# Feed-forward stages of a hybrid decoder step: from a scheduled order to a chain of slots in source order

## The chip, the cores and the metric

One core of a Trainium2 chip. The metric is the device time of one execution in microseconds (us), the median of the runs shown; lower is better.

## What is computed

One decoder layer for 1024 prompt tokens and 8 sampled tokens (1032 columns, D_MODEL = 1024, D_FF = 2816), in float32. The layer is a pair of half-step feed-forward stages around a mixer (attention and a state-space scan) and a cross attention:

```python
def swiglu(x, w_gate, w_up, w_down):
    return (jax.nn.silu(x @ w_gate) * (x @ w_up)) @ w_down

x = x + 0.5 * swiglu(rms_norm(x, g_ffn1), w1_gate, w1_up, w1_down)
...
x = x + 0.5 * swiglu(rms_norm(x, g_ffn2), w2_gate, w2_up, w2_down)
```

The change touches the two feed-forward stages alone.

## The kernel before

Everything lies transposed: features on the partitions, tokens on the free axis. The 1032 tokens are cut into P0 and P1 of 388 and a rest R of 256. `ffn` (both stages call it) walks through the 22 hidden blocks of 128 in pairs: a **gate-up unit** for an even block m, one for the odd block m + 1, then a **down unit** that adds both blocks into the residual x. The last pair has no down unit of this kind: `down_last` does it.

Each matrix product is made in Strassen's (Winograd's) form over P0 and P1: seven products of 388 columns instead of eight, on the weight matrices A11, A12 (gate weights), A21, A22 (up weights) and the sums S1 to S4 of them, with the factors B11 to B22 and T1 to T4 of the activations. The rest R is multiplied plainly by the four A matrices. Each product is made of three float32r matmuls (`three`): high half times high half, high times low, low times high. So a product of a gate-up unit is 12 matmuls of 388 columns, the rest of one matrix 12 matmuls of 256; a pair of blocks with its down unit has 396 matmuls: 252 of 388 columns and 144 of 256.

A weight matrix goes this way: `raw_` loads 512 KB by a DMA on SP's queue into a ring of two tiles (`fraw`); `add_up` makes the sums on DVE (VectorE); `split` copies the high half on ACT (ScalarE) and takes the low half by a subtraction, in turn on DVE and POOL (GpSimd), into a ring of four tiles (`fw`). Results lie in two sets of four PSUM banks (`fb`), which units take in turn: three banks of P0 and P1 products (b1, b2, b3) and one of the rest. `evac` says what becomes of a bank. The **seed** is one of these: ACT copies b1 to b2 after A11's product, so that b2 goes on from it, while b1 goes on with A12's product; both must wait for the copy. The hidden activations are made by SiLU on ACT and a product on DVE, put into halves by `put` (ACT copy, then a subtraction on DVE or POOL), and read by the down unit as its factors.

The order on each engine is the work of a scheduler, which goes by its own timing; the order in the source is a preference. The order of products is the table ORDER: A11, S2, A12, S3, S1, S4, A22, A21; a down unit takes the table's rows in the order 0, 7, 4, 1, 2, 3, 5, 6 for two halves c of the columns, each with two bank sets in step.

Of the kernel before, what the change touches and what calls it, by code (L numbers as in the profile page):

```python
# [10 lines left out]
F32 = mybir.dt.float32  # L11
# [65 lines left out]
def tile_step(ctx, tc, a, o):  # L77
# [237 lines left out]
    def split(hl, src, like=lambda t: t):  # L315

        hi, lo = like(hl[0]), like(hl[1])
        st["turn"] = not st.get("turn")
        nc.scalar.copy(hi, src)  # L319
        (nc.vector if st["turn"] else nc.gpsimd).tensor_sub(lo, src, hi.bitcast(F32))  # L320
        return hl
# [19 lines left out]
    def ffn(x, F, wg, wu, wd, fin, turn, mid=None):  # L341
# [27 lines left out]
        def gate_up(m):  # L369
            q = m % 2  # L370
            g_, u_ = raw_(cols_of(wg, m * 128)), raw_(cols_of(wu, m * 128))
            t = {"A11": g_[:, :512], "A12": g_[:, 512:], "A21": u_[:, :512], "A22": u_[:, 512:]}
            bk, rb = bank_set()
            b1, b2, b3 = bk
            sums = sums_of(m)
            e = {}

            def mat(name):
                if name == "S2":
                    add_up("S1", t, sums[:, :512])  # L380
                if name in SUMS and name not in t:
                    add_up(name, t, sums[:, :512] if name == "S3" else sums[:, 512:1024])
                return split(two(512), t[name])

            def rest(name, w):
                i = name in ("A21", "A22")
                first, last = name in ("A11", "A22"), name in ("A12", "A21")
                for j in range(4):
                    three(rb[:, int(i)], w, j, F["R"][j + (4 if name in ("A12", "A22") else 0)], first and j == 0, last and j == 3)

            def rest_end():
                gr, hr = u1_(NR), u1_(NR)
                nc.scalar.activation(gr, rb[:, 0], AF.Silu)
                nc.vector.scalar_tensor_tensor(hr, rb[:, 1], 0.5, gr, op0=OP.mult, op1=OP.mult)
                put(Hd["R"][q], hr, nc.vector)

            def evac(name):
                if name == "A11":
                    nc.scalar.copy(b2, b1)
                elif name == "S2":  # L400
                    e["U2"] = acc_(PA)
                    nc.scalar.copy(e["U2"], b2)
                elif name == "A12":
                    e["g0"] = g1_(PA)
                    nc.scalar.activation(e["g0"], b1, AF.Silu)
                elif name == "S3":
                    e["U3"] = acc_(PA)
                    nc.scalar.copy(e["U3"], b2)  # L408
                elif name == "S1":
                    e["u1"] = sq_(PA)  # L410
                    nc.vector.tensor_add(e["u1"], b3, e["U3"])  # L411
                elif name == "S4":
                    g1, u1 = g1_(PA), e["u1"]
                    nc.vector.tensor_add(g1, b3, e["U2"])
                    nc.scalar.activation(g1, g1, AF.Silu)
                    nc.vector.scalar_tensor_tensor(u1, u1, 0.5, g1, op0=OP.mult, op1=OP.mult)
                    if Hd["plain"]:
                        put(Hd["B22" if q else "B12"], u1, nc.vector)
                    elif q:
                        b12, t1 = Hd["b"]  # L420
                        nc.vector.tensor_sub(t1, u1, t1)
                        put(Hd["T2"], t1, nc.vector)
                        put(Hd["B22"], u1, nc.gpsimd)
                        nc.vector.tensor_sub(b12, u1, b12)
                        put(Hd["T3"], b12, nc.gpsimd)
                elif name == "A22":
                    u0, u1 = sq_(PA), e["u1"]
                    nc.vector.scalar_tensor_tensor(u0, b2, 0.5, e["g0"], op0=OP.mult, op1=OP.mult)
                    put(Hd["B21" if q else "B11"], u0, nc.vector)
                    if Hd["plain"]:  # L430
                        pass
                    elif q:
                        t2 = Hd["b"][1]
                        nc.vector.tensor_sub(u0, u0, t2)
                        put(Hd["T4"], u0, nc.gpsimd)
                    else:
                        nc.vector.tensor_sub(u0, u1, u0)
                        put(Hd["T1"], u0, nc.gpsimd)
                        Hd["b"] = (u1, u0)

            late = m == 0
            early = {}
            for name, b, f, first in ORDER:
                if late and name == "A21":
                    continue
                if name == "S3":
                    early["S1"] = mat("S1")
                w = early.pop(name, None) or mat(name)
                if f:
                    for j in range(4):  # L450
                        three(bk[b], w, j, F[f][j], first and j == 0, j == 3)
                if f:
                    evac(name)
                if name[0] == "A" and not late:
                    rest(name, w)
            if late:
                for name in ("A11", "A12", "A22", "A21"):
                    rest(name, mat(name))
            rest_end()

        def down(m0):
            ra, rb_ = (raw_(wd[m * 128:(m + 1) * 128]) for m in (m0, m0 + 1))
            sums = sums_of(1)
            twice = lambda t: t.rearrange("p (i c) -> p i c", i=2)
            for c in range(2):
                cs = slice(c * 256, (c + 1) * 256)
                wa, wb = twice(ra)[:, :, cs], twice(rb_)[:, :, cs]
                t = {"A11": wa[:, 0], "A21": wa[:, 1], "A12": wb[:, 0], "A22": wb[:, 1]}
                W = {}

                def pair(names, src):
                    hi, lo = split(two(512), src, twice if len(src.shape) == 3 else (lambda x: x))
                    for i, name in enumerate(names):
                        W[name] = hi[:, i * 256:(i + 1) * 256], lo[:, i * 256:(i + 1) * 256]

                def need(name):
                    if name in W:
                        return
                    if name in ("A11", "A21"):
                        pair(("A11", "A21"), wa)  # L480
                    elif name in ("A12", "A22"):
                        pair(("A12", "A22"), wb)
# [11 lines left out]
                def evac(name, e):  # L494
# [15 lines left out]
                    elif name == "A22":  # L510
                        add(xb[:, P0], xb[:, P0], b2)
# [1283 lines left out]
```

## Time and profile before

| | us |
|---|---|
| median of 3 runs (2667.94 to 2682.07) | 2678.17 |
| the profiled execution | 2680.7 |
| its span, first to last instruction | 2678.6 |
| PE busy in the span | 2508.9 (94%) |
| PE weight loads busy | 2384.3 (89%) |
| DVE, ACT, POOL busy | 1806.0, 1172.3, 906.3 |

The first feed-forward stage takes about 104 to 800 us of the span, the second about 1945 to 2640 us; between them lie the mixer and the cross attention. Times are microseconds from the start of the span. Matmuls overlap in the records: one of 388 columns is shown with 0.34 us, but the next starts sooner, so the pitch from start to start counts. Line numbers L... are those of the kernel before.

### The profile page before, as it was taken

The page shows a single profiled execution, that of the slowest core. Times are in us where ns is not written, and L with a number is a line of the kernel's source. Part 1 is how long each engine was busy: PE and PEld are TensorE (multiplying, and loading weights), DVE is VectorE, ACT ScalarE, POOL GpSimd, SP SyncE. Part 2 cuts the span into 40 slices and gives each one's busy share as a digit, 9 for nine tenths or more (in the row PEclk, how much of TensorE's full clock was granted, in tenths as well). Part 3 has the DMA queues.
Part 4 walks back from the last instruction along what each step waited for, and adds up shares of the span by engine and source line. Part 5 has one row for each costly group of instructions (what it writes and reads, how often), then busy time and mean ns, then how long its engine had stood idle before and what let it go on. Part 6 is the DMA issues. An engine that isn't in the chain of part 4 may idle for free.

```text
span 2678.6 us, 42139 instructions
## 1 busy us (share of the span) xinstructions
PE 2508.9 (94%) x15999; PEld 2384.3 (89%) x15999; DVE 1806.0 (67%) x3660; ACT 1172.3 (44%) x2415; POOL 906.3 (34%) x675
## 2 busy tenths in 40 slices
PE   6899999999999999999797899989699999999998
PEld 5899999999998899999576899978689999999997
DVE  8566666666656777778568877564876666666665
ACT  5443333333334455554467623333343333333345
POOL 5433333333334111115156564102443333333333
PEclk9999999999999999999898999999899999999999
DMA  5411111111113222327657634573011111111112
GB/s 172 135 50 64 57 57 58 61 59 57 57 48 112 81 70 65 92 75 239 201 167 221 221 108 132 169 236 104 23 48 48 48 48 49 55 48 52 51 48 80
DMA packets 273747, 252.12 MB, mean 94 GB/s; under 512 B 17392, under 2 KB 243880, under 8 KB 273536
## 3 DMA queue, kind: packets, MB, share of 16 engines
q1 hardware_dynamic: 271872, 249.34, 30.2%
q8 instruction: 126, 2.06, 0.3%
q14 instruction: 77, 0.63, 0.1%
q10 hardware_dynamic: 1672, 0.09, 0.0%
HBM read 204.25 MB, written 49.98 MB: 95 GB/s over the span
## 4 chain that ended last, share of the span: by engine, by line
PE 70%; DVE 15%; DMA 7%; issue 3%; ACT 3%; POOL 1%; SPq 0%; DVEq 0%; ACTq 0%; POOLq 0%
PE fb L332 44%; PE pqkv L245 5%; PE pxbc L245 4%; PE pcq L245 3%; DMA fraw<-in_w_up_dram 2%; PE pco L245 2%; PE pwa L245 1%; DVE fs L366 1%; PE pwo L245 1%; PE po L1071 1%; PE ps L1045 1%; PE ptr L1065 1%; PE pd L245 1%; PE pzz L245 1%; PE cps L1604 1%
## 5 line engine op out<-in xcount | busy, mean ns | idle before, releaser
L235 POOL TENSOR_TENSOR wl<-wr,wh 128x1024 fp32r<-128x1024 f32 (+4 forms) x79 | 166.1, 2103 | 562.1 <-ACT wh L231 537.2
L320 POOL TENSOR_TENSOR fw<-fraw,fw 128x512 fp32r<-128x512 f32 x131 | 174.2, 1330 | 465.8 <-ACT fw L319 392.4
L320 POOL TENSOR_TENSOR fw<-fs,fw 128x512 fp32r<-128x512 f32 x128 | 172.3, 1346 | 400.4 <-ACT fw L319 347.2
L319 ACT CAST fw<-fs 128x512 fp32r<-128x512 f32 x256 | 158.2, 618 | 268.5 <-PE fb L332 152.5
L319 ACT CAST fw<-fraw 128x512 fp32r<-128x512 f32 x262 | 162.2, 619 | 189.6 <-PE fb L332 185.9
L366 DVE TENSOR_TENSOR fs<-fraw 128x512 f32<-128x512 f32 (+1 forms) x168 | 101.0, 601 | 141.7 <-DMA fraw<-in_w_up_dram 67.0
L320 DVE TENSOR_TENSOR fw<-fraw,fw 128x512 fp32r<-128x512 f32 x131 | 102.5, 782 | 110.9 <-ACT fw L319 110.6
L320 DVE TENSOR_TENSOR fw<-fs,fw 128x512 fp32r<-128x512 f32 x128 | 95.5, 746 | 99.1 <-ACT fw L319 99.1
L332 PE MATMUL fb<-hRh,fw 128*128 128x256 f32 x640 | 137.3, 280 | 0.5
L231 ACT CAST wh<-wr 128x1024 fp32r<-128x1024 f32 (+1 forms) x80 | 76.8, 960 | 99.4 <-PE pqkv L245 23.4
L332 PEld LDWEIGHTS fb<-hRh,fw 128*128 128x128 f32 x640 | 109.2, 188 | 3.7 <-DVE x L516 3.7
L245 PE MATMUL pxbc<-xh,wh 128*128 128x344 f32 x288 | 94.0, 326 | 2.0 <-DVE xr L882 2.0
L245 PE MATMUL pqkv<-xh,wh 128*128 128x344 f32 x288 | 94.0, 326 | 0.4 <-DVE x L546 0.3
L245 PE MATMUL pxbc<-xl,wh 128*128 128x344 f32 x288 | 93.5, 324 | 0.0
L245 PE MATMUL pqkv<-xh,wl 128*128 128x344 f32 x288 | 93.1, 323 | 0.0
L245 PE MATMUL pqkv<-xl,wh 128*128 128x344 f32 x288 | 93.0, 323 | 0.0
L245 PE MATMUL pxbc<-xh,wl 128*128 128x344 f32 x288 | 92.9, 323 | 0.0
L332 PE MATMUL fb<-hRl,fw 128*128 128x256 f32 x320 | 87.6, 278 | 0.0
L411 DVE TENSOR_TENSOR tu<-fb,ts 128x388 f32<-128x388 f32 x44 | 24.7, 562 | 90.3 <-ACT ts L408 90.3
L1052 ACT ACTIVATE pr<-pr,nm 128x128 f32<-128x128 f32 (+3 forms) x64 | 49.7, 776 | 53.7 <-DVE nm L1050 53.3
L332 PE MATMUL fb<-T2h,fw 128*128 128x388 f32 x160 | 53.8, 357 | 17.1 <-ACT fb L499 17.1
L245 PE MATMUL pzz<-xh,wh 128*128 128x344 f32 x192 | 64.3, 335 | 4.1 <-DVE tv L914 2.2
(798 smaller groups left out, 9395.8 us busy)
## 6 DMA issues: line engine op xcount, KB each, us to landing
fraw<-in_w_gate_dram SPq DMA_DIRECT2D x44, 512.0 KB
fraw<-in_w_up_dram SPq DMA_DIRECT2D x44, 512.0 KB
fraw<-in_w_down_dram SPq DMA_DIRECT2D x44, 512.0 KB
wr<-in_w_in_dram SPq DMA_DIRECT2D x32, 512.0 KB
x_scr<-x SPq DMA_DIRECT2D x16, 516.0 KB
x<-x_scr SPq DMA_DIRECT2D x16, 516.0 KB
bc<-acs_scr SPq DMA_DIRECT2D x16, 512.0 KB
ckv<-in_cache_mem_k_dram SPq DMA_DIRECT2D x16, 512.0 KB
```

What stands on the lines that cost most here:

```text
L231: nc.scalar.copy(hi[:, :w], raw[:, :w])
L235: e.tensor_sub(lo[:, q], raw[:, q], hi[:, q].bitcast(F32))
L245: nc.tensor.matmul(ps, w, v, start=i == 0, stop=i == last)
L319: nc.scalar.copy(hi, src)
L320: (nc.vector if st["turn"] else nc.gpsimd).tensor_sub(lo, src, hi.bitcast(F32))
L332: nc.tensor.matmul(ps, l[:, js], m, start=bool(start and not i), stop=bool(stop and i == 2), skip_group_check=True)
L366: nc.vector.tensor_tensor(dst, t[p], t[q], op=op)
L1045: ins = nc.tensor.matmul(ps[:, c:c + n], qs[:, b * 128:w], kk[:, c:c + n], start=i == 0, stop=i == 1)
L1052: nc.scalar.activation(pr[:, :w], pr[:, :w], AF.Exp, scale=-1.0, bias=nm, accum_out=sm)
L1065: nc.tensor.transpose(p[:, j], pr[:, (c + j) * 128:(c + j + 1) * 128], ident)
L1071: nc.tensor.matmul(po[:, b % 2].rearrange("p i t -> p (i t)"), vv[:, j, e].rearrange("p i d -> p (i d)"), tts[j // 4][:, j % 4].rearrange( ...
L1604: nc.tensor.matmul(ps[:, u], l_[:, d, tk], r_[:, d], start=i == 0, stop=i == 5)
```

## The change

It replaces the scheduler's order within a feed-forward stage by one written out by hand. Each unit becomes a list of **slots**: a matrix to prepare (`mat` or `mats`), a piece of PE work, and the steps that empty banks afterwards (`evs`). The function `run` walks through all slots of all units: at slot i it first records the preparation of slot i + 3 (AHEAD = 3), then the PE work of slot i, then one waiting step of each earlier slot and the first step of slot i. All this stands within `tc.manual_schedule` for PE, DVE, ACT and POOL: what is recorded on one of these engines runs there in the order in which it was recorded. SP's queue is not among them.

The slots of a gate-up unit are A11, A12, S2, S1, S3, S4, A21, A22 (the up weights are needed from the third one on, for S2). A11 and A12 take their rest behind the product, A21 has a rest alone, A22 has its rest first and is closed by the product. A down unit has for each half four slots: `first` (A11's product for two sets, the seeds, the rests of A11 and A21), `sums12`, `sums34`, `final`. Block 0 leaves the rests to the end as before.

Three things more: in a down unit all subtractions of `split` go to POOL; its four sums are made by one call, ahead of the slot of S1 and S2; and the addition of bank b1 to x (`moved`) becomes a copy on ACT and an addition on POOL. So per pair DVE has 8 subtractions and 4 additions less, POOL 8 and 4 more, ACT 4 copies more. S1 of a gate-up unit is now copied by ACT and added to S3's bank on DVE, where before S3 was copied and S1 added.

```diff
-    ORDER = (("A11", 0, "B11", True), ("S2", 1, "T2", False), ("A12", 0, "B21", False), ("S3", 1, "T3", False),
-             ("S1", 2, "T1", True), ("S4", 2, "B22", False), ("A22", 1, "T4", False), ("A21", None, None, False))
...
+            def product(name, b, f, first, late):
+                def mm(w):
...
+                    if name in ("A21", "A22") and not late:
+                        rest(name, w)
+                    if f:
+                        for j in range(4):
+                            three(e["bk"][b], w, j, F[f][j], first and j == 0, j == 3)
+                    if name in ("A11", "A12") and not late:
+                        rest(name, w)
+                return mm
...
+            def seed():
+                nc.scalar.copy(e["bk"][1], e["bk"][0])
...
+            for name, b, f, first, evs in (
+                    ("A11", 0, "B11", True, (seed,)), ("A12", 0, "B21", False, (silu,)), ("S2", 1, "T2", False, (kept("U2", 1),)),
+                    ("S1", 2, "T1", True, (kept("s1", 2),)), ("S3", 1, "T3", False, (up1,)), ("S4", 2, "B22", False, (gate1, hid1, hid1b)),
+                    ("A21", None, None, False, ()), ("A22", 1, "T4", False, (hid0 if late else ends, hid0b))):
...
+                    if names[0] in SUMS:
+                        i = 0 if names[0] == "S1" else 2
+                        for j, nm in enumerate(() if i else ("S1", "S2", "S3", "S4")):
+                            add_up(nm, t, t["sums"][:, j * 256:(j + 1) * 256])
+                        hl = split(two(512), t["sums"][:, i * 256:(i + 2) * 256], eng=nc.gpsimd)
...
+                def moved(x_, b):
...
+                    t_ = acc_(PA)
+                    nc.scalar.copy(t_, b)
+                    nc.gpsimd.tensor_add(x_, x_, t_)
...
+                def first(W, c=c, U=U):
...
+                    for e in U:
+                        three(e["b"][0], W[0], e["j"], Hd["B11"], True, True)
+                        nc.scalar.copy(e["b"][1], e["b"][0])
+                    for i in range(2):
+                        for e in U:
+                            three(e["r"][:, i], W[i], e["j"], Hd["R"][0], i == 0, False)
...
+                for names, mm in ((("A11", "A21"), first), (("S1", "S2"), sums12), (("S3", "S4"), sums34), (("A12", "A22"), final)):
+                    out.append((lambda names=names, mats=mats: mats(names), mm, ()))
...
+        AHEAD = 3
...
+            for i in range(-AHEAD, len(slots)):
+                if i + AHEAD < len(slots):
+                    W[i + AHEAD] = slots[i + AHEAD][0]()
...
+                mm(W.pop(i))
+                todo, left = left, []
+                for evs_ in todo + [evs]:
+                    if evs_:
+                        evs_[0]()
+                        left.append(evs_[1:])
...
+        with tc.manual_schedule(engines={E_.PE, E_.DVE, E_.Activation, E_.Pool}):
+            run(units)
```

Two places show what moves; both are of the second pair (blocks 2 and 3). The first is ACT at the border from the even to the odd gate-up unit. Names: `fw` a split weight, `tg` gate values, `tv` and `hRh` the rest's hidden values, `tu` hidden values, `fb_1265` and `fb_1266` the odd unit's b1 and b2. Before:

```order
L393 ACTIVATE tv_2098<-fb_1272 128x256
L319 CAST fw_2138<-fs_1497 128x512
L264 CAST hRh_1910<-tv_2099 128x256
L319 CAST fw_2155<-fraw_2104 128x512
L415 ACTIVATE tg_2045<-tg_2045 128x388
L319 CAST fw_2184<-fs_1497 128x512
L264 CAST B11h_1896<-tu_2064 128x388
L399 COPY fb_1266<-fb_1265 128x388
L319 CAST fw_2188<-fs_1497 128x512
L264 CAST T1h_1906<-tu_2064 128x388
```

With the change:

```order
L429 ACTIVATE tg_2068<-tg_2068 128x388
L321 CAST fw_2071<-fraw_2049 128x512
L321 CAST fw_2089<-fs_1457 128x512
L403 ACTIVATE tv_2116<-fb_1272 128x256
L264 CAST B11h_1924<-tu_2120 128x388
L321 CAST fw_2124<-fs_1457 128x512
L264 CAST hRh_1938<-tv_2117 128x256
L264 CAST T1h_1934<-tu_2120 128x388
L410 COPY fb_1266<-fb_1265 128x388
L321 CAST fw_2158<-fs_1457 128x512
```

The seed (the copy to `fb_1266`) stood ahead of T1's copy and now stands behind it; the even unit's rest is read (L403) behind the SiLU of its gate (L429), where before it was read first.

The second place is DVE at the border from the odd gate-up unit to the down unit. `fb_1268` is the odd unit's rest bank, `fraw` the raw down weights, `fs` their sums. Before:

```order
L320 TENSOR_TENSOR fw_2281<-fraw_2106,fw_2281 128x512
L411 TENSOR_TENSOR tu_2217<-fb_1267,ts_2203 128x388
L366 TENSOR_TENSOR fs_1497<-fraw_2303,fraw_2305 128x256
L366 TENSOR_TENSOR fs_1497<-fs_1497,fraw_2303 128x256
L366 TENSOR_TENSOR fs_1497<-fraw_2305,fs_1497 128x256
L394 SCALAR_TENSOR_TENSOR tv_2297<-fb_1268,tv_2296 128x256
L320 TENSOR_TENSOR fw_2332<-fs_1497,fw_2332 128x512
```

With the change:

```order
L428 TENSOR_TENSOR tg_2258<-fb_1267,ts_2203 128x388
L364 TENSOR_TENSOR fs_1457<-fraw_2239,fraw_2241 128x256
L364 TENSOR_TENSOR fs_1457<-fs_1457,fraw_2239 128x256
L364 TENSOR_TENSOR fs_1457<-fraw_2239 128x256
L364 TENSOR_TENSOR fs_1457<-fraw_2241,fs_1457 128x256
L433 SCALAR_TENSOR_TENSOR tu_2237<-tu_2237,tg_2258 128x388
L438 TENSOR_TENSOR tu_2120<-tu_2237,tu_2120 128x388
L265 TENSOR_TENSOR T2l_1931<-tu_2120,T2h_1930 128x388
L445 TENSOR_TENSOR tu_2047<-tu_2237,tu_2047 128x388
L404 SCALAR_TENSOR_TENSOR tv_2317<-fb_1268,tv_2316 128x256
L450 SCALAR_TENSOR_TENSOR tu_2320<-fb_1266,tg_2185 128x388
L265 TENSOR_TENSOR B21l_1927<-tu_2320,B21h_1926 128x388
```

The reading of the rest bank `fb_1268` stood ahead of the hidden values of the odd block; now the four sums, which need both raw down weights, and four steps on those hidden values stand ahead of it.

## Rows read from the trace of the kernel before

**Rows 1.** The page: busy time, share of the span and instructions of each engine.

```profile
PE 2508.9 (94%) x15999; PEld 2384.3 (89%) x15999; DVE 1806.0 (67%) x3660; ACT 1172.3 (44%) x2415; POOL 906.3 (34%) x675
```

**Rows 2.** Two pairs, middle: us; busy PE PEld DVE ACT POOL; PEclk; DMA; GB/s.

```profile
235.00:299.20 64.20, 62.34 (x396) 61.60 (x396) 41.07 (x80) 24.92 (x50) 20.11 (x16) 1.00 0.19 59
2072.50:2136.40 63.90, 63.23 (x396) 61.55 (x396) 41.80 (x80) 24.97 (x50) 20.69 (x17) 1.00 0.17 50
...
800.00:1945.00 1145.00, 1047.29 (x6811) 962.98 (x6811) 819.21 (x1796) 542.30 (x1179) 390.86 (x270) 0.95 0.44 135
```

**Rows 3.** Chain of waits: start, us, what; first stage, then second stage.

```profile
170.72 55.32 PE fb L332 x348
...
292.43 4.36 DMA fraw<-in_w_up_dram
...
298.12 0.56 DVE x L511
299.21 56.85 PE fb L332 x348
...
753.26 45.27 PE fb L332 x283
...
2072.54 46.09 PE fb L332 x291
...
2519.68 46.06 PE fb L332 x291
```

**Rows 4.** A stretch from 299.2 us on, columns as in rows 2.

```profile
299.20:303.00 3.80, 3.79 (x16) 3.79 (x17) 2.78 (x6) 0.43 (x1) 0.00 (x0) 0.55 0.00 0
```

**Rows 5.** Instructions of PE and SP in order of time: start, us, engine, line.

```profile
400.10 0.34 PE L332 MATMUL fb<-T11h,fw 128*128 128x388 f32 x1
...
400.28 0.33 PE L332 MATMUL fb<-T11l,fw 128*128 128x388 f32 x1
...
403.35 0.34 SPq L325 DMA_DIRECT2D fraw<-in_w_down_dram  x1
...
404.20 0.29 PE L332 MATMUL fb<-R5h,fw 128*128 128x256 f32 x1
...
404.32 0.28 PE L332 MATMUL fb<-R5l,fw 128*128 128x256 f32 x1
```

**Rows 6.** Instructions of ACT and DVE in order of time, 404 to 412 us.

```profile
404.05 0.48 ACT L408 COPY ts<-fb 128x388 f32<-128x388 f32 x1 [1.48 <-PE fb L332]
404.43 0.62 ACT L319 CAST fw<-fraw 128x512 fp32r<-128x512 f32 x1
...
406.93 0.38 ACT L393 ACTIVATE tv<-fb 128x256 f32<-128x256 f32 x1 [1.88 <-PE fb L332]
407.09 0.42 DVE L366 TENSOR_TENSOR fs<-fraw 128x256 f32<-128x256 f32 x1 [1.97 <-DMA fraw<-in_w_down_dram]
...
411.05 0.53 ACT L415 ACTIVATE tg<-tg 128x388 f32<-128x388 f32 x1
```

**Rows 7.** Instructions of DVE, POOL and ACT, 2097 to 2105 us.

```profile
2097.10 0.68 DVE L366 TENSOR_TENSOR fs<-fs,fraw 128x512 f32<-128x512 f32 x1
...
2100.03 1.54 POOL L320 TENSOR_TENSOR fw<-fs,fw 128x512 fp32r<-128x512 f32 x1 [0.17 <-ACT fw L319]
...
2100.80 1.31 DVE L366 TENSOR_TENSOR fs<-fraw,fs 128x512 f32<-128x512 f32 x1
...
2102.51 0.55 DVE L265 TENSOR_TENSOR B11l<-tu,B11h 128x388 fp32r<-128x388 f32 x1
...
2104.30 0.51 ACT L264 CAST T1h<-tu 128x388 fp32r<-128x388 f32 x1
2104.43 0.69 DVE L320 TENSOR_TENSOR fw<-fs,fw 128x512 fp32r<-128x512 f32 x1 [0.29 <-ACT fw L319]
```

**Rows 8.** PE at the start of each stage: first wait for S2's product.

```profile
111.79 0.69 PE L332 MATMUL fb<-T20h,fw 128*128 128x388 f32 x1 [2.89 <-ACT fb L399]
...
1948.04 0.67 PE L332 MATMUL fb<-T20h,fw 128*128 128x388 f32 x1 [3.49 <-ACT fb L399]
```

More of the change, by code (lines that the diff above doesn't have):

```diff
@@ L370, in gate_up @@
             q = m % 2
[L371 to L376, printed above, removed]
-            def mat(name):
[L379 to L382, printed above, removed]
+            t, e, out = {}, {}, []
+            def mat(name):
+                if not t:
+                    g_, u_ = raw_(cols_of(wg, m * 128)), raw_(cols_of(wu, m * 128))
+                    t.update(A11=g_[:, :512], A12=g_[:, 512:], A21=u_[:, :512], A22=u_[:, 512:], sums=sums_of(m))
+                if name in SUMS:
+                    sums = t["sums"]
+                    for nm in {"S2": ("S1", "S2"), "S1": ()}.get(name, (name,)):
+                        add_up(nm, t, sums[:, :512] if nm in ("S1", "S3") else sums[:, 512:1024])
                 return split(two(512), t[name])
@@ L386, in rest @@
                 i = name in ("A21", "A22")
-                first, last = name in ("A11", "A22"), name in ("A12", "A21")
+                first, last = name in ("A11", "A21"), name in ("A12", "A22")
                 for j in range(4):
-                    three(rb[:, int(i)], w, j, F["R"][j + (4 if name in ("A12", "A22") else 0)], first and j == 0, last and j == 3)
-            def rest_end():
[L392 to L439, printed above, removed]
@@ new lines, in rest @@
+                    three(e["rb"][:, int(i)], w, j, F["R"][j + (4 if name in ("A12", "A22") else 0)], first and j == 0, last and j == 3)
+            def product(name, b, f, first, late):
+                def mm(w):
+                    if not e:
+                        e["bk"], e["rb"] = bank_set()
+                    if name in ("A21", "A22") and not late:
[6 more added lines that the diff above has]
+                return mm
@@ new lines, in hid1b, with hid0 @@
+            def hid1b():
+                if q and not Hd["plain"]:
+                    b12, u1 = Hd["b"][0], e["u1"]
+                    put(Hd["B22"], u1, nc.gpsimd)
+                    nc.vector.tensor_sub(b12, u1, b12)
+                    put(Hd["T3"], b12, nc.gpsimd)
+            def hid0():
+                u0 = e["u0"] = sq_(PA)
+                nc.vector.scalar_tensor_tensor(u0, e["bk"][1], 0.5, e["g0"], op0=OP.mult, op1=OP.mult)
+                put(Hd["B21" if q else "B11"], u0, nc.vector)
@@ L444, in gate_up @@
                 if late and name == "A21":
                     continue
[L446 to L455, printed above, removed]
+                out.append((lambda name=name: mat(name), product(name, b, f, first, late), evs))
@@ L456, in gate_up @@
             if late:
-                for name in ("A11", "A12", "A22", "A21"):
-                    rest(name, mat(name))
-            rest_end()
+                for name in ("A11", "A12", "A21", "A22"):
+                    out.append((lambda name=name: mat(name), lambda w, name=name: rest(name, w),
+                                (rest_end, rest_end2) if name == "A22" else ()))
+            return out
         def down(m0):
-            ra, rb_ = (raw_(wd[m * 128:(m + 1) * 128]) for m in (m0, m0 + 1))
@@ L463, in down @@
[L463 removed]
+            out, raws = [], []
             twice = lambda t: t.rearrange("p (i c) -> p i c", i=2)
             for c in range(2):
[L466 to L482, printed above, removed]
[L483 to L523 removed]
@@ L549, in ffn, with hidden @@
         last = DFF // 128 - 2
-        for m in range(0, DFF // 128, 2):
+        def hidden(m):
             for nm in MATS if m < last else ("B11", "B12", "B21", "B22"):
```

165 lines of the change are left out of this document (112 added, 53 removed).

## The prediction

> **What bounds the kernel now.** I read the page first for who is busy: TensorE (PE) has 94% of the span, DVE 67%, POOL 34% [rows 1]. So only PE's gaps can be gained, and new gaps are what can be lost. Then the stretches of one pair of hidden blocks in each stage, to see how much gap there is: PE's weight loads, which don't overlap each other in the records, sum to 61.60 and 61.55 us for 396 matmuls [rows 2]. The pitch from start to start agrees: 0.18 us at 388 columns and 0.12 at 256 [rows 5], 252 × 0.177 + 144 × 0.12 = 61.9. So 61.6 us is the dense time of a pair, and it does not change, since the change issues the same matmuls.
>
> Third, the chain of waits, for the true period. Its PE pieces repeat: in the first stage from 170.72 to 753.26 in nine pairs, 64.73 us each; in the second from 2072.54 to 2519.68 in seven, 63.88 us each [rows 3]. So the kernel before loses 3.1 us per pair in stage one and 2.3 in stage two. All that the change can gain inside the pairs is 10 × 3.1 + 10 × 2.3 = 54 us (ten full pairs a stage; the eleventh I leave unchanged).
>
> The chain also shows what the loss of stage one is: PE stands for S2, the second product of a unit, whose up weights arrive by a DMA of 4.36 us [rows 3]. In one pair the granted clock after such a wait is 0.55 of full speed for 3.8 us, so part of it at the lower level, 1.2 GHz [rows 4], and that piece of the chain is 56.85 us instead of 55.32 [rows 3]: 1.5 us on top of the wait.
>
> **The change, part by part.**
>
> *Up weights used third.* Between A11 and S2 now lies A12 too, product 12 × 0.177 = 2.12 and rest 12 × 0.12 = 1.44 us. That covers the wait of stage one, and most of the first wait of each stage, 2.89 and 3.49 us [rows 8]. I take -2 us for each start (between 0 and -3.5), and let the in-pair wait go wholly: if nothing new came, a pair would take 61.6 plus some border loss.
>
> *Engine load.* Eight subtractions of 0.69 us [rows 7] and four additions, by the nearest row 0.42 each [rows 6], leave DVE: -7.2 us of some 41 [rows 2]. They go to POOL at about 1.26 each (20.11 us over 16 instructions [rows 2]): +10 for the subtractions, up to +5 for the additions, so 30 to 35 of 62 us busy. ACT gets four copies of 0.48 [rows 6], +2 to 25. None becomes the bound by its load; what hides it is that each is busy well under 61.6 us. The order is the matter: each engine now runs in the order of the source, and a step stands behind whatever was recorded ahead of it. I walked through one pair by the order rows, with durations of rows 6 and 7: DVE and ACT hand over in about 0.03 us, a bank is readable 0.2 after its last matmul, and successive steps of one engine overlap by about 0.1. Four places are late.
>
> 1) *The seed of the odd gate-up unit.* The seed is the last of a chain that starts at the end of the even unit's S4: gate 0.55, SiLU 0.53, cast of A12 0.62, its subtraction 0.69, hidden value 0.55, the sums S1 and S2 0.68 each, cast 0.62, rest's SiLU 0.38, its product 0.42, second hidden value 0.55, copy of B11 0.51, cast 0.62, subtraction 0.69, rest's low half 0.42, T1 difference 0.55, its copy 0.51, seed 0.48: 10.05 us, plus 0.6 for readability and handing over, less 0.8 of overlap: 9.85 [rows 6, 7]. PE gets there after A21 (1.44), A22 (3.56) and the next A11 (3.56), 8.56 us after S4. Stall **1.3 us** (1.0 to 1.6).
>
> 2) *The rest bank of the odd block.* The down unit's `first` needs it for its second set. From the end of S1: copy 0.48, cast of A22 0.62, subtraction 0.69 that frees the raw tile, the second down matrix from its issue on SP to the first sum 403.35 to 407.09 = 3.74 [rows 5, 6], four sums 1.45 (each 0.42, overlapped): 7.2. Then hidden value, T2 difference, copy, T3 difference, copy, rest's SiLU and product as in the order rows: 11.2. PE comes after 2.12 + 2.12 + 1.44 + 3.56, and 1.42 in `first`: 10.66. So 0.55 at least; the sums stand beside POOL's subtractions, and if they are held up there, as below, 1.9. I take **1.4**, nearer to the upper end, since four sums in a row meet a POOL that is busy half the time.
>
> 3) *`sums34`.* Its B22 goes on in b2, whose reader on DVE waits behind the rest's product, the second hidden value, and the low halves of B21 and of the rest: some 4.1 us from the rest's product, against 3.2 of PE's work. Stall 0.9, to 1.6 with POOL in the way; **1.1**.
>
> 4) *`final`.* T4 on b1 waits for T3's additions, which stand behind the four sums of the next half. By the same steps 0.4 (no collision) to 1.6; **0.9**. Nothing in the trace of before has this order, so its low end may be nil.
>
> The adds of `moved` on POOL have nobody on PE waiting for x within the unit: nothing. In the second half of the columns and at the odd-to-even border I find PE busy for longer than the steps take: nothing, at the cover of 8 to 10 us that PE's work gives there.
>
> *DVE beside POOL.* A POOL subtraction runs from 2100.03 for 1.54 us; a DVE sum starting beside it at 2100.80 takes 1.31, where the same instruction alone took 0.68 [rows 7]. So it ends just after POOL ends. The Trainium skill (SBUF — State Buffer, "Who interferes with whom") calls this an exclusive lock on a shared pair of ports, held for the whole instruction, so the loser fully blocks; the trace agrees, 1.31 against 0.68. The same notes (Perfetto Trace Analysis, on optimizing Scalar/DVE operations) warn that offloading between those two might therefore not help; if every sum here met the lock, the pair would be the 68.3 us of rival D, 2754 in all, against the forecast's 66.3.
>
> By the row alone I reckon with a collision in about half of the cases, since POOL will be busy half of the time, and have put terms 2 to 4 between their ends for that.
>
> **Sum.** 1.3 + 1.4 + 1.1 + 0.9 = 4.7 us per pair (1.0 + 0.55 + 0.9 + 0 = 2.45 to 1.6 + 1.9 + 1.6 + 1.6 = 6.7), on 61.6: 66.3 us. Against 64.73 and 63.88 that is 10 × 1.6 + 10 × 2.4 = +40, less 4 for the two starts: +36. The middle, 1145 us with PE idle in 98 of it [rows 2], is also scheduled a little differently, since the scheduler's order there changes with what precedes it; I take 0 ± 10, a tenth of that idle time. The profiled execution took 2680.7 us, 2.5 above the median of the runs, so 2680.7 + 36 - 2.5 gives **2714** as the median.
>
> **The rivals.**
>
> A, *the feeders keep up*: the four chains turn out shorter than I walk them (matrices prepared earlier, no collision), and PE loses 0.8 us per pair. For it: the wait that bounds stage one is on the up weights, which come later now; DVE has 7 us less. Against: the seed's chain of 18 steps, with no free slot in it. Then 62.4 us: -23 - 15 - 4 = -42, **2636**; with no loss at all 61.6: -31 - 23 - 4 = -58, 2620.
>
> B, *an even trade*: the four waits are there at their lower ends, 2.45 to 3.6 us per pair, and pay back what the up weights' wait gave: 64.05 to 65.2 us, so -9 to +14: **2669 to 2692**.
>
> C, *the clock*: a wait of PE is followed by the lower clock, as at 299.20 [rows 4]. At 1.5 us [rows 3] and one such per pair: 20 × 1.5 = +30 on the forecast, **2744**. The wait in the trace that did it was one of about 2 us; my four are 1.9 at the most, which speaks against.
>
> D, *every collision on POOL*: terms 2 to 4 and the seed at their upper ends, 6.7 per pair, 68.3 us: +36 + 44 - 4 = +76, **2754**. It decides once each of DVE's sums and low halves that stand in these chains meets a POOL subtraction. Against it: POOL is busy half the time.
>
> **How the numbers follow.** The forecast (3.6 to 5.6 us per pair, 2692 to 2733) has 0.40, since each of the four waits follows from the order alone, though their sizes rest on a walk by hand; A 0.27, because such a walk adds up every small error in one direction; B 0.18; C 0.07; D 0.08. About 0.5%, 13 us, is what a measurement of this kernel can tell from no change, so "same" is 2665 to 2691: B, 0.18. Faster is A, 0.27; slower is the forecast with C and D, 0.55. The likeliest case's own range is 2692 to 2733. The range that is to hold 8 in 10 takes in it, B, C, the upper two thirds of A and a part of D: 2630 to 2750.
>
> **What would show it.** Right: the chain of waits shows PE for S2 without the up weights' DMA ahead of it; PE waits on ACT's seed for about 1.3 us before the odd unit's A12, and on DVE before `first`'s second rest, `sums34` and `final`; the stretch of one pair is 66 us with 61.6 of weight loads and clock 1.00; POOL 30 to 35 us per pair, DVE about 34, with single sums of 1.3. Wrong: a pair of 62 to 63 us (A), in which case I walked a chain too long, most likely term 2 with its DMA; or a granted clock under 1 in most pairs (C). If the middle differs by over 10 us, the sum fails there and not in the pairs.

## The result, and the profile after

The changed kernel takes 2790.32 us (median of 4 runs, 2787.41 to 2796.49) beside 2676.68 us: a ratio of 1.0431 with an interval of 1.0397 to 1.0464. That is 114 us slower; 36 had been forecast, and the range ended at 2750.

Its page, busy time by engine (it answers to [rows 1]):

```profile
PE 2516.5 (90%) x15999; PEld 2391.8 (86%) x15999; DVE 1769.9 (64%) x3500; ACT 1205.1 (43%) x2495; POOL 1088.8 (39%) x835
```

PE does the same work in a longer span, 2784.8 us for 2678.6. From the start of a stage's first product to that of its last matmul (of `three`), in us:

| | before | after | difference |
|---|---|---|---|
| stage one | 106.6 to 799.1 | 107.8 to 836.7 | +36.4 |
| between the stages | 1141.2 | 1138.6 | -2.6 |
| stage two | 1940.3 to 2630.8 | 1975.3 to 2741.2 | +75.4 |
| ahead and behind | 106.6, 47.9 | 107.8, 43.7 | -3.0 |

The middle hardly moves. Line numbers are from here on those of the kernel whose trace is shown. Counted from one even unit's first matmul to the next one's, over nine pairs, a pair goes from 64.73 to 68.41 us in stage one and from 63.94 to 71.52 in stage two. The stretches of single pairs, two of each stage (columns as in [rows 2]):

```profile
178.24:246.47 68.23, 63.24 (x396) 62.01 (x396) 39.72 (x72) 26.57 (x54) 30.13 (x24) 1.00 0.16 49
451.98:520.60 68.62, 63.26 (x397) 62.03 (x397) 39.75 (x72) 26.57 (x54) 30.09 (x24) 1.00 0.18 55
2055.79:2126.45 70.66, 63.01 (x399) 61.64 (x398) 39.84 (x72) 26.60 (x53) 29.43 (x25) 1.00 0.15 45
2126.45:2198.72 72.27, 64.50 (x398) 63.10 (x397) 40.06 (x72) 26.60 (x53) 29.44 (x25) 0.98 0.14 44
```

PE is busy as before and stands still for 5 us of a pair in stage one, over 7 in stage two. In 5 of stage two's nine pairs the granted clock is 0.98 on the mean, and those are 1.5 us longer. POOL has 30 us, the low end of the forecast; but DVE, which was to fall from 41 to 34, has 39.7. The counts say why in part: per pair DVE has 72 steps for 80 and POOL 24 for 16 [rows 2]. So 8 steps moved and not the 12 of the section on the change: the down unit's eight subtractions took turns before, and four of them were POOL's already. Four subtractions and four additions left DVE. Where PE stands, from the matmuls of one pair in each stage (start, us, instruction, in brackets the idle time ahead and its releaser):

```profile
478.43 0.44 PE L334 MATMUL fb<-B210h,fw 128*128 128x388 f32 x1 [1.13 <-ACT fb L410]
...
498.95 0.38 PE L334 MATMUL fb<-hRh,fw 128*128 128x256 f32 x1 [1.75 <-DVE tv L404]
...
503.56 0.45 PE L334 MATMUL fb<-B22h,fw 128*128 128x388 f32 x1 [1.14 <-DVE x L509]
...
508.90 0.41 PE L334 MATMUL fb<-T4h,fw 128*128 128x388 f32 x1 [1.19 <-ACT ts L514]
...
2125.63 0.39 PE L334 MATMUL fb<-hRh,fw 128*128 128x256 f32 x1 [1.21 <-DVE x L509]
...
2153.03 0.69 PE L334 MATMUL fb<-B210h,fw 128*128 128x388 f32 x1 [2.31 <-ACT fb L410]
```

The first four are the four waits of the prediction, in its order: the seed ahead of the odd unit's A12, the odd block's rest bank, B22 in `sums34`, T4 in `final` (it counts a set's banks from 0: its b2 and b1 there are the third and the second bank). For T4 the record names ACT's copy of the first bank, which came last, at 508.86 us; DVE's first addition of T3, which the prediction named, was done at 508.77, and both stand behind the second half's four sums. The last two are stage two's: a second rest that waits for an addition (stage one has hardly any of it), and the seed wait doubled; the matmul behind that took 0.69 us for 0.44. The seed wait is 2.29 to 2.31 us in all nine pairs, but the granted clock falls behind it in five only.

Why the stages differ is in the subtractions. DVE, POOL and their neighbours ahead of the seed, first stage one, then stage two:

```profile
470.40 0.69 DVE L322 TENSOR_TENSOR fw<-fraw,fw 128x512 fp32r<-128x512 f32 x1 [1.10 <-ACT fw L321]
...
471.48 0.69 DVE L364 TENSOR_TENSOR fs<-fraw 128x512 f32<-128x512 f32 x1
...
476.55 0.42 DVE L265 TENSOR_TENSOR hRl<-tv,hRh 128x256 fp32r<-128x256 f32 x1
...
2143.96 1.30 POOL L322 TENSOR_TENSOR fw<-fraw,fw 128x512 fp32r<-128x512 f32 x1 [3.52 <-ACT fw L321]
2144.27 1.53 DVE L364 TENSOR_TENSOR fs<-fraw 128x512 f32<-128x512 f32 x1 [0.30 <-DMA fraw<-in_w_up_dram]
...
2150.27 1.30 DVE L265 TENSOR_TENSOR hRl<-tv,hRh 128x256 fp32r<-128x256 f32 x1 [0.27 <-ACT hRh L264]
```

The low half of A12 is DVE's in stage one and POOL's in stage two, and in stage two two steps of the seed's chain run beside POOL's and take 1.53 for 0.69 and 1.30 for 0.42 us. `split` alternates between the engines by a flag that nobody sets back. Block 0 makes 7 + 4 = 11 splits and each of the other 21 blocks 8, so a stage makes 179, an odd number: stage two starts with the flag reversed.

### The profile page after: what moved, and what is told of

Same layout as the page of the kernel before. It is cut to its first block, busy times and chain, and to the rows that moved or that the text cites. A ratio compares the mean times of both kernels' runs of the same rounds, so it can differ in the third digit from the quotient of the medians.

```text
span 2784.8 us, 42357 instructions
## 1 busy us (share of the span) xinstructions
PE 2516.5 (90%) x15999; PEld 2391.8 (86%) x15999; DVE 1769.9 (64%) x3500; ACT 1205.1 (43%) x2495; POOL 1088.8 (39%) x835
## 4 chain that ended last, share of the span: by engine, by line
PE 53%; DVE 23%; DMA 8%; ACT 8%; issue 6%; POOL 1%; SPq 1%; DVEq 0%; ACTq 0%; POOLq 0%
PE fb L334 28%; PE pqkv L245 5%; PE pxbc L245 4%; DVE fs L364 4%; PE pcq L245 3%; ACT fw L321 3%; DMA fraw<-in_w_down_dram 3%; DVE x L509 2%; PE pco L245 2%; PE pwa L245 1%; DVE hRl L265 1%; DVE tu L438 1%; PE pzz L245 1%; PE ps L1103 1%; PE po L1129 1%
## 5 line engine op out<-in xcount | busy, mean ns | idle before, releaser
L322 POOL TENSOR_TENSOR fw<-fs,fw 128x512 fp32r<-128x512 f32 x168 | 226.1, 1351 | 435.7 <-ACT fw L321 387.7
L322 POOL TENSOR_TENSOR fw<-fraw,fw 128x512 fp32r<-128x512 f32 x171 | 227.8, 1332 | 310.0 <-ACT fw L321 309.9
L509 DVE TENSOR_TENSOR x<-x,fb 128x388 f32<-128x388 f32 (+1 forms) x560 | 249.9, 512 | 24.5 <-PE fb L334 24.5
L322 DVE TENSOR_TENSOR fw<-fraw,fw 128x512 fp32r<-128x512 f32 x91 | 66.0, 725 | 243.5 <-ACT fw L321 241.5
L364 DVE TENSOR_TENSOR fs<-fraw 128x512 f32<-128x512 f32 (+1 forms) x168 | 127.5, 759 | 40.0 <-DMA fraw<-in_w_down_dram 19.0
L322 DVE TENSOR_TENSOR fw<-fs,fw 128x512 fp32r<-128x512 f32 x88 | 68.7, 781 | 122.9 <-ACT fw L321 122.8
L515 POOL TENSOR_TENSOR x<-x,ts 128x388 f32<-128x388 f32 x80 | 86.1, 1098 | 35.4 <-ACT ts L514 35.4
L415 ACT COPY ts<-fb 128x388 f32<-128x388 f32 x88 | 42.5, 483 | 110.5 <-PE fb L334 110.5
```

Of the source, the lines that this page charges most:

```text
L322: eng.tensor_sub(lo, src, hi.bitcast(F32))
L364: nc.vector.tensor_tensor(dst, t[p], t[q], op=op)
L415: nc.scalar.copy(e[name], e["bk"][b])
L509: nc.vector.tensor_add(x_, x_, b)
L515: nc.gpsimd.tensor_add(x_, x_, t_)
```

## The experiments

Unless a diff says otherwise, each is an edit of the changed kernel. Where nothing else is said a time is that of one run; it is compared by its span with 2784.8 us, or by its time with that of the kernel before on the same chip (2679 to 2681 us).

**The phase of the alternation, set back and reversed.**

```diff
         AHEAD = 3
+        st["turn"] = False
```

This is e1_turn; p1_flip has True in its place.

> The edit sets the DVE/POOL alternation of the gate-up subtractions back at the start of each feed-forward stage, so that stage two gives each matrix to the same engine as stage one. Theory (the alternation comes out of stage one reversed, since block 0 makes 11 splits): a pair of stage two falls from 71.6 us to stage one's 68.4, seed wait 2.3 to 1.2 us, no wait of the rest on x, granted clock 1.00 in each pair; in all -32 us, about 2758. Rival (stage two is slower for another reason, such as its DMA or the clock after the mixer): no change, 2790.

> The opposite of e1_turn: the alternation is set at each stage's start so that stage one gets the order of engines that stage two has in the changed kernel. If the phase alone makes the 3 us a pair between the stages: stage one's pairs rise from 68.4 to 71 to 72 us with a seed wait of 2.3 us, stage two stays at 71.5; about +30, 2815 to 2825. If the stages differ by something else as well (and e1_turn helped stage two by chance): stage one stays under 70, 2790 to 2800.

e1_turn: 2750.7 us, span 2748.9, 36 less. Pairs of stage two 67.88 us, clock 1.00 in all nine. p1_flip: 2816.0 us; pairs of stage one 71.60, stage two 71.58. PE's waits in 200 to 800 us of p1_flip (engine, line, waited for: us in total, times, longest), that is in stage one:

```profile
PE fb L334 <- ACT fb L410: 20.2, 9, 2.5
PE fb L334 <- DVE x L509: 17.0, 14, 1.3
PE fb L334 <- DVE tv L404: 16.6, 8, 2.2
PE fb L334 <- ACT ts L514: 9.3, 8, 1.2
```

and of the changed kernel in the same stretch:

```profile
PE fb L334 <- DVE tv L404: 13.8, 9, 1.8
PE fb L334 <- ACT ts L514: 10.8, 9, 1.2
PE fb L334 <- DVE x L509: 10.7, 11, 1.2
PE fb L334 <- ACT fb L410: 10.5, 9, 1.4
```

The flag makes either stage slow or less slow, with the same waits: stage two is 36 us shorter in e1_turn, stage one 31 longer in p1_flip. It is 36 us of the 106 between the two profiled executions.

**Order by hand or the work's place.**

```diff
-        with tc.manual_schedule(engines={E_.PE, E_.DVE, E_.Activation, E_.Pool}):
-            run(units)
+        run(units)
```

> The changed kernel without the manual schedule: slots, engines and arithmetic as changed, but the scheduler orders each engine as in the kernel before. If the order by hand is the cause of the loss: the pairs come back to 63 to 66 us, 2660 to 2710. If what is at fault is the work's place (eight subtractions and four additions on POOL beside DVE, four sums at once, the products' order), which this kernel keeps: 2760 or more.

2699.8 us, 19 above the kernel before: the order by hand makes some 90 of the 114, or 83 of the 112 by which the two stages are longer. The phase's 36 are among them: this kernel has the reversed flag in stage two as well, and its pairs there take 65.6 us, those of stage one 66.0. Then the shift to POOL undone as well (m1):

```diff
-                        hl = split(two(512), t["sums"][:, i * 256:(i + 2) * 256], eng=nc.gpsimd)
+                        hl = split(two(512), t["sums"][:, i * 256:(i + 2) * 256])
...
-                        hl = split(two(512), t["wa" if names[0] == "A11" else "wb"], twice, eng=nc.gpsimd)
+                        hl = split(two(512), t["wa" if names[0] == "A11" else "wb"], twice)
...
-                                moved(e["x"][0][:, P0], e["b"][0])
+                                add(e["x"][0][:, P0], e["b"][0])
```

and the four sums at once undone too (m2):

```diff
-                        for j, nm in enumerate(() if i else ("S1", "S2", "S3", "S4")):
-                            add_up(nm, t, t["sums"][:, j * 256:(j + 1) * 256])
+                        for j, nm in enumerate(("S3", "S4") if i else ("S1", "S2")):
+                            add_up(nm, t, t["sums"][:, (i + j) * 256:(i + j + 1) * 256])
```

> As e4_no_manual (scheduler), and the shift to POOL is undone too: the down unit's subtractions take turns again, b1 is added to x by DVE. What is left of the change: the order of the products with its slots and the four sums at once. If the 17 us that e4_no_manual is slower than the kernel before come from POOL (steps of DVE held up beside it, 5 to 6 us a pair): 2665 to 2675, as fast as the kernel before with its up weights third. If they come from the slots and the sums: 2690 to 2700.

> As m1_sched_undo, and the four sums at once are undone too: S3 and S4 are made ahead of their own slot. What is left of the change is the order of products with its slots. If the sums make the rest of the loss: 2670 to 2678. If it is the slots' order: within 4 us of m1_sched_undo's 2687.

m1: 2687.2 us, m2: 2681.9 us, 8 and 1 above the kernel before beside them, each between what its two theories expected. In the totals the sums are worth some 7 us and nothing remains. The stages say otherwise (in us, the last column against the kernel before):

| | stage one | middle | stage two | both stages |
|---|---|---|---|---|
| before | 692.5 | 1141.2 | 690.5 | |
| changed | 728.9 | 1138.6 | 765.8 | +111.8 |
| e4_no_manual | 705.3 | 1136.6 | 706.1 | +28.5 |
| m1_sched_undo | 700.3 | 1133.3 | 701.8 | +19.2 |
| m2_sched_need | 700.7 | 1128.3 | 701.1 | +18.9 |

m2's total comes level because its middle, whose source no edit touches, is 13 us shorter. Two runs of one and the same kernel (the next experiment's) differ by 4 us in the stages and by 6 in the middle. So POOL is about 9 us, the sums at once are worth nothing that can be told, and some 19 us stay in the stages with the products' order and its slots, though a scheduler places the steps. Which part of the slots costs them is not shown.

**The products' order alone, in the kernel before.**

```diff
-    ORDER = (("A11", 0, "B11", True), ("S2", 1, "T2", False), ("A12", 0, "B21", False), ("S3", 1, "T3", False),
+    ORDER = (("A11", 0, "B11", True), ("A12", 0, "B21", False), ("S2", 1, "T2", False), ("S3", 1, "T3", False),
```

The down unit's order of products stays (its indices are exchanged with the rows).

> The kernel before with the change's order of two products alone: A12 ahead of S2, so that the up weights are needed from the third product on; scheduler and all else as before. If the wait of stage one (1.9 us a pair idle, and the lower clock behind three of nine) is on the up weights' arrival alone: it goes, -20 to -25 us, about 2656. Rival (the wait moves to the next product that needs S1 or S3, since DVE's sums are late anyway): within 8 us of 2681.

> The kernel g1_before_third once more, timed in five rounds. Its one look was 11 us faster than the kernel before beside it (0.4%). If the order of the products alone is worth that: a ratio of 0.995 to 0.997 with an interval under 1; if it was the middle or chance: an interval that holds 1.

One run gave 2668.2 us beside 2679.2; twelve gave a ratio of 0.9988, interval 0.9974 to 1.0002: no gain that can be told from none, and no loss, so this exchange by itself is not what costs the 19 us above. The waits of stage one stayed (14.4 us against 16.5 before, in nine pairs), and where they lie shows a mistake of mine. PE in the kernel before:

```profile
493.55 0.44 PE L332 MATMUL fb<-T2h,fw 128*128 128x388 f32 x1 [1.86 <-ACT fb L499]
```

`T2h` without a number is a factor of the down unit. PE stood there for the down unit's seed, not for a gate-up product: DVE held a sum that waited for the up weights, and behind it in its queue the addition that frees the seed's bank [rows 3].

**The steps' order.** A slot's own first step ahead of older ones (e2):

```diff
-                for evs_ in todo + [evs]:
+                for evs_ in [evs] + todo:
```

Preparation behind the slot's work (e3), by moving these lines to the end of the loop's body for i of 0 and more:

```diff
-                if i + AHEAD < len(slots):
-                    W[i + AHEAD] = slots[i + AHEAD][0]()
```

S3 and S4 of a down unit made later (e7, the diff of m2 alone), and the down unit's subtractions in turn again (e5, the two lines of m1 with `split`).

> The edit lets a slot's own first step be recorded ahead of the waiting steps of earlier slots, so the seed stands ahead of T1's difference and copy, and the reading of the rest ahead of T3's. Order theory: the seed's wait goes (1.4 us a pair in stage one, 2.5 and the clock's loss of 0.8 in stage two), the wait for the rest bank shrinks by some 1.1 us: -25 and -44, about 2722. Lock theory (the waits come from POOL work beside DVE, wherever the steps stand): the time comes back in the next wait, less than 20 us gained, 2770 or more.

> The edit records the preparation of slot i + 3 behind the PE work and the steps of slot i instead of ahead of them. Order theory: T3's additions no longer stand behind four sums, so the wait before T4 in the first half goes (1.4 us a pair), the hidden value of the odd block no longer stands behind sums that wait for the down weights' DMA (0.5 or more at the rest bank), and the seed's chain loses sums and a cast (1.4 or more): -3 us a pair, -60 in all, about 2730. Rival (preparation is what is short, three slots are needed in full): weights come late, PE waits on DVE or POOL for fw instead, 2790 or more.

> The edit undoes one part: of the four sums of a down unit's half only S1 and S2 are made ahead of their slot, S3 and S4 ahead of theirs. Order theory: two sums of 0.42 us less ahead of the rest bank's reader and of T3's additions, and with them up to one collision with POOL (0.9): 0.8 to 1.7 us a pair at each of the two waits, -16 to -50 in all, about 2760. Rival (the rest wait is set by the DMA of the second down matrix alone): the wait for the rest bank stays at 1.8 and only the one before T4 shrinks, -10 to -20, about 2775.

> The edit undoes one part: the subtractions of a down unit's split take turns on DVE and POOL again. Lock theory: with half of POOL's work at the border gone, DVE's held-up steps there (four of them, 3.2 us together in a pair of stage one) run at their own length, and this outweighs four subtractions of 0.69: 10 us faster or more in all. Order theory: the chain on DVE gets those subtractions added, two or three of them ahead of a waiting bank: slower by 1 to 2 us a pair, 2810 to 2830. The alternation's phase does not change by it (eight splits a down unit).

e2: 2758.0 us, between its two theories; its gain is all in stage two (pairs of 69.1 us), stage one stays at 68.2. In nine pairs of stage one the seed's wait goes from 10.5 us to nothing and the rest's from 13.8 to 4.8, but a new one of 10.4 stands behind them, for the down unit's seeds, and B22's grows from 10.4 to 13.7. e3: 2799.5 us, a miss. T4's wait is gone, as expected, but the seed's is 3.3 us, and pairs of stage one have a granted clock of 0.95. e7: 2789.4 us, outside both ranges: nothing. In nine pairs of stage one T4's wait falls from 10.8 us to 4.5 and the rest's stays at 13.8. For the rest neither edit does what was expected of it: in e7 the two sums only move down, to 494.40 and 494.73 us in one pair, and in e3 all four stand at 512.80 to 513.93, each time still ahead of T3's difference and so of the rest's reader. What the sums cost at the rest bank is not shown. e5: 2830.2 us, 40 slower: pairs of stage one 68.7, stage two 75.2. DVE can't take that work in this order, though most steps beside it are held up less. So I read the waits as one chain, of which PE meets the first late bank. The chain of waits of the changed kernel from the down weights towards T4 (start, us, what; ten pieces of it):

```profile
488.34 3.93 DMA fraw<-in_w_down_dram
...
492.85 1.10 DVE fs L364 x3
493.95 0.48 DVE tu L433
...
494.45 1.55 DVE tu L438
...
498.48 0.42 DVE tv L404
498.90 0.48 DVE tu L450
...
501.56 0.99 DVE hRl L265
502.56 0.47 DVE tu L464
503.03 1.87 DVE x L509 x4
504.90 1.33 DVE fs L364
```

From 492.4 us to T4's release at 508.9 DVE and ACT hand one chain to and fro.

**The border's chain, shortened.** All with e1's flag and e2's order: f1 alone; h1 with a down unit's four sums recorded behind the slot's steps; k1 with those of the second half alone and with b2 of the odd unit read a slot later; k3 as k1, but with b2 read in its own slot and only its copy later.

```diff
-                    ("A21", None, None, False, ()), ("A22", 1, "T4", False, (hid0 if late else ends, hid0b))):
+                    ("A21", None, None, False, ()), ("A22", 1, "T4", False, (hid0, hid0b) if late else (rest_end, hid0, hid0b))):
```

That is k1; in k3 the middle step holds `put` alone, and the product that reads b2 stands at the end of `hid1b`. In h1 and the later two the preparation of the down unit's S1 and S2 stands behind the slot's steps, as in e3:

```diff
+                if behind:
+                    W[i + AHEAD] = slots[i + AHEAD][0]()
```

> Both edits at once: the alternation set back at each stage's start, and a slot's own first step ahead of older ones. Order theory, each wait by itself: the gains add up but for the seed's, which both took from stage two: 2749 - 29 + 5, about 2725, a pair 67 to 68 us in both stages with no wait on the odd gate-up unit's seed. Chain theory (the waits at the border from the odd unit to the down unit are one backlog on DVE that PE meets at whichever bank comes first): the sum of the border's waits stays at 4.1 us and more, and only the seed's 1.4 us a pair is gained: about 2720 too, but with waits at the down unit's seed, B22 and T4 that add up to what PE came earlier.

> As f1_turn_own, and the four sums of a down unit's half are recorded behind the PE work and the steps of the slot in which they are prepared (behind the odd block's hidden value in the first half, behind T3's additions in the second). Chain theory: DVE no longer stands for the DMA with ready work behind it and the wait before T4 goes (1.4 us): a pair 65 to 66 us, 2690 to 2705. Lock theory (DVE's work at the border is long because POOL's subtractions hold it up, order only shifts where PE waits): within 10 us of f1_turn_own.

> As f1_turn_own, with two moves at the border from the odd unit to the down unit: A22's step is split, so that in its own slot only the rest is read and the hidden value of b2 with its copy (B21) comes one slot later, behind the down unit's seeds; and the four sums of the second half are recorded behind T3's additions. Chain theory: the down unit's seeds (1.2 us in f1_turn_own) wait on ACT behind B21's copy, which waits for the end of A22's product; B21 and T4 are needed last, so putting them behind costs nothing, and seeds, B22 and T4 lose their waits: 2.5 to 4 us a pair, 65 us or less, about 2690. Rival (PE's waits at this border are set by the amount of work on DVE, 12 us and more between S4 and T4, held up by POOL): the wait moves to B21 or T4 and the pair stays at 67, about 2740.

> As k1_split_hid0, but b2 of the odd unit is still read (by DVE) in A22's slot, behind T3's steps, as it must be before the down unit's second seed overwrites that bank; only the copy and the low half of B21 come a slot later. Chain theory: one true dependency is back on the path (read of b2 0.55 us behind A22's end, then the seeds): a pair 66.5 to 67 us, 2715 to 2730, still under f1_turn_own's 2740. Rival (the lower clock behind the waits takes it back): pairs with a granted clock of 0.95 to 0.98 and 2740 or more.

f1: 2740.5 us, pairs 67.97 and 67.10, no wait on the gate-up seed; the gains of e1 and e2 don't add up, and both expectations were too low. h1: 2777.1 us, a miss: the down unit's seeds wait 2.0 us, and 16 of 18 pairs have a granted clock of 0.95 to 0.98 and are 1.3 us or more longer than its best, 67.2. The seeds stand on ACT behind copies that need A22's end; in k1 and k3, which take B21's copy from there, they no longer wait. k1: 2713.2 us; it reads b2 after the down unit's seed has overwritten it, so the odd blocks' hidden values of that bank are others. k3, with the read in its place: 2713.1 us, pairs 66.72 and 66.06. Its waits in 200 to 800 us:

```profile
PE fb L334 <- DVE x L517: 24.5, 27, 2.3
PE fb L334 <- DVE tv L404: 3.5, 9, 0.6
```

28.0 us for 45.8 in the changed kernel. Two moves are in k3 at once (B21's copy and the second half's sums), and no run tells which gained. Seeds and T4 are gone from the list; what is left is PE waiting for DVE's additions to x. No version by hand came under the kernel before.

## Why the prediction was wrong

**The sign and the four places were right**: seed, rest bank, `sums34`, `final`, forecast with 1.3, 1.4, 1.1 and 0.9 us; their means over nine pairs of stage one are 1.17, 1.53, 1.16 and 1.20. The mechanism is shown for the seed, which has no wait once it stands ahead of T1's copy (e2); for T4, whose wait halves with two sums fewer ahead (e7); and for a part of the rest's, 1.0 us of 1.53, once its reader stands ahead of T3's steps (e2). B22's was only argued. The time was 114 us longer and not 36. Between the profiled executions, which lie 106 us apart, 70.2 are missing: 36.4 are term 1, 33.2 terms 2 and 3 (1.6 to 2.1 us in each of 18 pairs), 6.2 the first pairs and the stages' ends (term 5), less 5.6 outside the stages.

1. *One walk for both stages* (the largest). The four waits were priced once and multiplied by twenty. The alternation's flag comes out of stage one reversed, which the order rows of one pair of stage one cannot show. Measured 36 us, the clock in stage two with it. The count of 179 splits was there to be made.

2. *The base of 61.6 us and the price of a wait.* I took the weight loads' sum for the dense time and added the waits' idle time. But a wait costs more than its idle time: the start at 478.43 lies 1.42 us behind the one before it, where the pitch is 0.12, and the next follows after 0.28 instead of 0.18. So 1.30 + 0.10 = 1.40 us are lost with 1.13 idle: 0.27 on top, 1.1 us for four waits. And the kernel before had 64.27 us in an undisturbed pair of stage one with one wait of 1.86, which cost 0.27 more as well: that leaves 62.1 and not 61.6. With 0.5 of base, 1.1 for the waits' ends, and 5.1 us of idle (45.8 in nine pairs) for 4.7, the 66.3 become 68.3, beside 68.4 measured.

3. *DVE's relief.* "-7.2 us" was wrong twice. Eight steps left DVE and not twelve: four subtractions of 0.69 and four additions of 0.55, 5.0 us; POOL came to 30 us with eight steps more where twelve had been priced, which is luck: the additions took 1.06 us each there, and the price for them had been anything up to 5 us. And of the 5.0 the sum of DVE's durations shows 2.1 in stage one and 2.9 in stage two, the busy time of a pair 1 to 2: steps with two operands in SBUF ran longer beside POOL than they had before. In stage two of the changed kernel (form, times, us in total, mean ns):

```profile
L364 DVE TENSOR_TENSOR fs<-fraw 128x256 f32<-128x256 f32 x32 | 21.2, 663 | 8.3 <-DMA fraw<-in_w_down_dram 8.3
L265 DVE TENSOR_TENSOR hRl<-tv,hRh 128x256 fp32r<-128x256 f32 x16 | 18.3, 1142 | 5.7 <-ACT hRh L264 5.7
L438 DVE TENSOR_TENSOR tu<-tu 128x388 f32<-128x388 f32 x8 | 12.3, 1537 | 0.3
...
L445 DVE TENSOR_TENSOR tu<-tu 128x388 f32<-128x388 f32 x8 | 4.4, 556 | 0.0
```

L438 and L445 are the same operation on the same sizes: 1537 and 556 ns. L438 starts beside a POOL subtraction that is under way (start, us; a pair of stage one):

```profile
494.09 1.48 POOL L322 TENSOR_TENSOR fw<-fs,fw 128x512 fp32r<-128x512 f32 x1 [3.39 <-ACT fw L321]
494.45 1.54 DVE L438 TENSOR_TENSOR tu<-tu 128x388 f32<-128x388 f32 x1
```

The three upper groups alone lost (663 - 420) × 32 + (1142 - 420) × 16 + (1537 - 556) × 8 = 27 us in eight pairs against their undisturbed length. The Trainium skill (SBUF — State Buffer, "Who interferes with whom") says that a DVE instruction with two SBUF inputs contends with a GpSimd instruction that reads SBUF, while one with at most one SBUF input outside the 2-port modes does not; these numbers agree, and the additions to x, with one input in PSUM, stayed at 551 ns. Yet rival D, every collision met, is not what happened in stage one: that its 68.3 us a pair stand beside 68.4 is chance, for the waits there add up to 5.1 us and not 6.7. Taking the subtractions back made the kernel slower (e5). I read it so: the lock sets the length of the chain, the order sets that PE waits for it; no run takes the collisions away and leaves the order, so this division is argued.

4. *The clock.* C was put at "one per pair" and 0.07. In stage one no pair lost by it; in stage two 5 of 9 did, 1.5 us each, right behind the seed wait of 2.3, the wait I had missed. The argument that shorter waits are safe does not hold in general: in e2 three pairs of stage one have a granted clock of 0.95 with no wait over 1.54 us.

5. *What the kernel before waited for.* I put the wait of [rows 3] at a gate-up unit's S2. It was at the down unit's seed, and the up weights came into it through DVE's queue. The step "most of the first wait of each stage goes" fell too: 2.83 us at 112.91 and 4.21 at 1983.54, now ahead of A12 for the seed, where [rows 8] had 2.89 and 3.49; the first pairs are 2.9 and 6.9 us longer, not 2 shorter.

Rivals A and B fell with the waits found. What stays open: the 19 us of the slots in the stages, and whether an order by hand with yet fewer additions on DVE at the border can pass the scheduler's.

## What to carry to other kernels

When every engine runs in source order, walk the chain once for each place where the code's state differs (flags, rings, parity), not once for each unit that looks alike, and count the flips. Price a wait of PE at its idle time plus what is lost as it stops and starts, here some 0.3 us. Count which engine has a step now before you price its move to another. Where an engine is one long chain at a border, cutting one wait mostly moves PE to the next: shorten the chain, or leave its order to the scheduler, which here was worth 83 us in the stages. And compare a change by the stages it touches: a shorter middle hid 13 us of a loss here.

## What the runs showed that I had not expected

A flag that alternates two engines moved 31 to 36 us of a stage by its phase alone (2750.7, 2790 and 2816 us with two, one and no stage in the better phase). And the granted clock fell behind some waits and not behind others: in e1_turn, whose waits in stage two are at most 1.5 us, all nine pairs have 1.00; h1_lastsum, with waits of 2.0 us at the seeds in each pair, has 0.95 to 0.98 in 16 of 18 pairs and gains nothing by its later sums. f1_turn_own had some such pairs with waits of up to 1.5 and 2.0 us, and in the changed kernel the seed wait of 2.3 us is followed by the lower clock in five pairs and not in four, so no length of wait separates them cleanly here.
